# A two-layer diffusion step on TensorE: moving operands placed 16 bytes further on relative to the weights

## The chip, the cores and the metric

The kernel runs on one core of a Trainium2 chip, as one program in one launch. The metric is the device time of one execution in microseconds (us). A core has engines that run side by side: TensorE (PE in the profile; its weight loads are a row of their own, PEld), VectorE (DVE), ScalarE (ACT), GpSimd (POOL) and SyncE (SP), which issues the DMAs here.

## The reference

One inference step of a hybrid backbone of two layers, width 2048, for two groups of 128 tokens each: a context pass (`x_prompt`) and a denoising step (`x_sample`, which also attends to 128 cached keys). Both groups use the same weights, so the kernel carries them side by side as 256 columns.

```python
for l in range(DEPTH):                                   # DEPTH = 2
    mod = silu(cond) @ w_ada[l] + b_ada[l]               # 2048 x 12288
    sh1, sc1, gt1, sh2, sc2, gt2 = split(mod, 6)
    h = rmsnorm(x, g_norm_mix[l]) * (1 + sc1) + sh1
    x = x + gt1 * (mixer_ab(h) if l == 0 else mixer_c(h))
    h = rmsnorm(x, g_norm_ffn[l]) * (1 + sc2) + sh2
    x = x + gt2 * conv_ffn(h)
y = rmsnorm(x, g_final)
```

`mixer_ab` is multi-head latent attention beside grouped-query attention, with one input and one output projection. `mixer_c` is differential attention with eight heads. `conv_ffn` projects up to 2 x 5632 columns, convolves over three neighbouring tokens, multiplies the SiLU of one half with the other and projects down to 2048. All arrays are float32.

## The kernel before

Every weight matrix is cut into blocks of 128 x 128. A block arrives from memory as float32 in a tile `raw`, and `split` (lines 220 and 221) makes two tiles of it: ScalarE casts it to `wh` in the rounded format float32r, VectorE subtracts and writes the rest as `wl`. Activations are split in the same way into a high and a low half. A chunk product (`gemm`, lines 313, 314 and 317; `first_three`, lines 299 to 301, for the first three chunks after a norm) adds up three matmuls for each block: `wh` with the high half, `wh` with the low half, `wl` with the high half. The weights are the stationary operand, the activations the moving one, 256 columns of 4 bytes each time (384 in the products of latent keys and values). Each matmul has a weight load of its own, which runs beside the matmul before it.

The moving operands of all chunk products are five kinds of tiles:

- `hx`, 16 rows of 512 values (high half, low half) per partition: the normed and modulated input of each mixer and ConvFFN, and as `o` the heads' output of the first mixer (pool `keep`);
- `kv_in` and `ql`, latent keys and values and latent queries of the first mixer (pool `ab`);
- `oall`, the differential heads' output of the second mixer (pool `cc`);
- `g`, 22 tiles of 512 values, the gated product between the projections of the ConvFFN (pools `ffn0`, `ffn1`).

The weights `wh` and `wl` lie in four tiles each of 1024 values in the pool `wpool`, which follows `keep`. Tiles are allocated in the order in which their names first appear, at multiples of 32 bytes of each partition. Tiles named `pad` set where the next ones begin: 48 values ahead of the tiles of `wpool`, `SHIFT // 4` = 112 values ahead of `kv_in` and of the ConvFFN's tiles, `SHIFT // 4 - 24` ahead of `oall`. With them every moving tile starts 448 bytes (`SHIFT`) behind the weights, counted in a period of 512 bytes; rows, halves and blocks are multiples of 512 bytes apart.

The order of the work on each engine comes from a planner that simulates the program when it is built, apart from what is held in program order by hand. Between the chunk products a helper `pump` places the products for the modulation vectors (line 427 on TensorE, line 404 on VectorE) and steps of the attention heads. The chunk products of the two ConvFFN layers are the two long stretches (490 to 1215 us and 1650 to 2374 us); the first mixer lies before the one, the second mixer before the other.

```python
    T_(wpool, [P, 48], "pad", bufs=1)
    ...
                T_(ab, [P, SHIFT // 4], "pad")
                kv_in = T_(ab, [P, 4, 2, 3 * T], "kv_in", F32R)
    ...
        T_(cp, [P, SHIFT // 4 - 24], "pad")
        o_all = T_(cp, [P, KD, ROW], "oall", F32R)
```

Of the kernel before, what the change touches and what calls it, by code (L numbers as in the profile page):

```python
# [11 lines left out]
F32R = mybir.dt.float32r  # L12
# [6 lines left out]
P = 128  # L19
D = 2048  # L20
KD = D // P
T = 128
NT = 2 * T
ROW = 2 * NT
SHIFT = 448
NL = 2
GRID_W = 64
EPS = 1e-6
# [5 lines left out]
KQ = NFF // NQ  # L34
# [50 lines left out]
def step_kernel(ctx: ExitStack, tc: tile.TileContext, A: dict):  # L85
# [24 lines left out]
        return pl.tile(shape, dt, tag=tag, name=nm(tag), **kw)  # L110


    T_(wpool, [P, 48], "pad", bufs=1)


    cst = T_(keep, [P, NCONST], "cst")
# [410 lines left out]
    def modulated(st, l, which, W, fixed):  # L527


        ensure(l, 3 * which + 1)  # L530
        ensure(l, 3 * which)
        while later:
            later.pop(0)()
        u = ROWS[ada["i"]]
        tile_ = lambda t: T_(wpool, [P, 4, 512], "araw", bufs=2)

        def load_tile(t):
            raw = tile_(t)
            sp.dma_start(out=raw, in_=A["w_ada"][u[0], u[1], u[2], t])
            return raw  # L540

        raws = [load_tile(0), load_tile(1)]
        hx = T_(keep, [P, KD, ROW], "hx", F32R)
        r = stat_rstd(st, D, att_bank)
        sum_rows(0, raws[0], bank())
        rb = spread(diagonal(r, (0, 1)), bank=att_bank)
        sum_rows(1, raws[1])
        raws += [load_tile(2), load_tile(3)]
        modulate(hx, rb, l, which, range(KD), fixed)
        ada["i"] += 1  # L550
        rest = ada_finish(*u)

        def last_rows():
            sum_rows(3, raws[3])
            rest[0]()

        def turn():
            rest[1](tc.keep_in_program_order)

        ps = first_three(W, lambda k: hx[:, k, :NT], lambda k: hx[:, k, NT:2 * NT],  # L560
                         AS_MADE if fixed else IN_TURN, lambda: sum_rows(2, raws[2]), fixed)
        if fixed:
            W.ahead(lambda i: i)
        return hx, ps, [last_rows, turn]
# [72 lines left out]
    def mixer_ab(hx, rb0, st):  # L637
        l = 0
        with tc.tile_pool(name="ab", bufs=1) as ab:
            with tc.tile_pool(name="abp", bufs=1) as pj:  # L640
                T_(ab, [P, SHIFT // 4], "pad")
                kv_in = T_(ab, [P, 4, 2, 3 * T], "kv_in", F32R)
                ckc = T_(pj, [P, 4, T], "ckc")
                kr = T_(ab, [P, 3 * T], "kr")
                kg = T_(ab, [P, 2, 3 * T], "kg")
# [7 lines left out]
                    tc.keep_in_program_order(sp.dma_start(out=vg[:, 1], in_=A["cache_gqa_v"]))  # L653


                ql = T_(ab, [P, 6, 2 * NT], "ql", F32R)
                qb = T_(ab, [P, 8, NT], "qb")
                rsb = T_(ab, [P, 8, 2], "rsb")
                rsm = T_(ab, [P, 2], "rsmla")
# [131 lines left out]
            with tc.tile_pool(name="abh", bufs=1) as hp:  # L791
                ada["pew"] = PEW["heads"]

                o = T_(keep, [P, KD, ROW], "hx", F32R)
                load_cw(0)
                WQ = Weights(A["w_q_up"], 6, 2)
                WK = Weights(A["w_kv_up"], 4, 4)
                qh, qlo = (lambda k: ql[:, k, :NT]), (lambda k: ql[:, k, NT:])
                kh, klo = (lambda k: kv_in[:, k, 0]), (lambda k: kv_in[:, k, 1])
                qn, qr = {}, None  # L800

                def gqa_query(h):
                    s2 = T_(tmp, [P, NT], "sq", bufs=2)
                    act.activation(s2, qb[:, h], AF.Square)
                    act.activation(qb[:, h], qb[:, h], AF.Identity, scale=C("gqn"))
                    yield
                    pst = T_(pmisc, [P, 512], "misc")
                    for g in range(2):
                        pe.matmul(pst[:, g:g + 1], s2[:, g * T:(g + 1) * T], inv(128),
                                  start=True, stop=True)  # L810
                    rstd([pst[:, 0:2]], 2, HEAD_SCALE, rsb[:, h])
                    rope(qb[:, h:h + 1, T:], qb[:, h:h + 1, T:], 1, 64, "rch", "rsh")

                def gqa(h):
                    k = kg[:, h // 4]
                    return head_ab(hp, [(qb[:, h], k)], rsb[:, h], lambda b: vg[:, b, h // 4], o, 8 + h)

                def mla(h, qnh, qrh, knh, vh):
                    half = slice(64 * (h % 2), 64 * (h % 2) + 64)
                    return head_ab(hp, [(qnh, knh), (qrh[half], kr[half])], rsm,  # L820
                                   lambda b: vh[:, b], o, h)

                flush()
                start(gqa_query(0))
                for h in range(8):
                    if h % 2 == 0:
                        for i in range(2):
                            ps = gemm(WQ.chunk(), qh, qlo)
                            qn[h + i] = T_(hp, [P, NT], "qn", bufs=4)
                            act.copy(qn[h + i], ps)  # L830
                            pump(RATE["heads"])
                        ps = gemm(WQ.chunk(), qh, qlo)
                        ev = T_(tmp, [P, NT], "nt", bufs=4)
                        act.copy(ev, ps)
                        qr = T_(hp, [P, NT], "qr", bufs=2)
                        act.copy(qr[:, 0:T], ev[:, 0:T])
                        rope(qr[:, None, T:], ev[:, None, T:], 1, 32, "rcm", "rsm")
                        pump(RATE["heads"])
                    if h < 7:
                        start(gqa_query(h + 1))  # L840
                    start(gqa(h))
                    ps = gemm(WK.chunk(), kh, klo, 3 * T)
                    kn = T_(hp, [P, 3 * T], "kn", bufs=2)
                    act.copy(kn, ps)
                    pump(RATE["heads"])
                    ps = gemm(WK.chunk(), kh, klo, 3 * T)
                    vt = T_(hp, [P, 3 * T], "vt", bufs=2)
                    act.copy(vt, ps)
                    pump(RATE["heads"])

                    def values_and_head(h, vt, *a):
                        pt = T_(ppool["att"], [P, 512], "att", bufs=3)
                        for b in range(3):
                            pe.transpose(pt[:, b * T:(b + 1) * T], vt[:, b * T:(b + 1) * T], ident)
                        vm = T_(hp, [P, 3, P], "vm", bufs=2)
                        act.copy(vm.rearrange("p b d -> p (b d)"), pt[:, :3 * T])
                        yield
                        yield from mla(h, *a, vm)

                    start(values_and_head(h, vt, qn[h], qr, kn))  # L860
                flush()
# [11 lines left out]
    def mixer_c(cp, hx, W, ready, todo, st):  # L873
# [11 lines left out]

        xh, xl = (lambda k: hx[:, k, :NT]), (lambda k: hx[:, k, NT:2 * NT])
        product = lambda: ready.pop(0) if ready else gemm(W.chunk(), xh, xl, between=todo.pop(0) if todo else None)
        T_(cp, [P, SHIFT // 4 - 24], "pad")
        o_all = T_(cp, [P, KD, ROW], "oall", F32R)

        def project(h):
            q = T_(cp, [P, 2, NT], "dq", bufs=2)
# [103 lines left out]
    def ffn(hx, W, ready, todo, l, st):  # L996
# [4 lines left out]
        with tc.tile_pool(name=f"ffn{l}", bufs=1) as fp, banks(f"pffn{l}") as pf:  # L1001
# [22 lines left out]
            def up(q):  # L1024
                gs = []
                for i in range(q * KQ, (q + 1) * KQ):
                    rate = 0 if i < LATE else FRATE["up"]
                    fine[0] = False
                    gate = conv(i)
                    pump(0, rate)  # L1030
                    val = conv(NFF + i)
                    pump(0, rate)
                    act.activation(gate, gate, AF.Silu)
                    dve.tensor_tensor(out=val, in0=gate, in1=val, op=ALU.mult)
                    g = T_(fp, [P, ROW], "g", F32R, bufs=KQ)
                    split(g[:, :NT], g[:, NT:2 * NT], val)
                    gs.append(g)
                    if l == 0 and i == LATE - 1:
                        load_row()
                return gs  # L1040
# [18 lines left out]
    with banks("pab") as ppool["ada"]:  # L1059
        ppool["att"] = ppool["ada"]  # L1060
        for c in range(0, KD, 4):
            sp.dma_start(out=x[:, c:c + 4], in_=A["xT"][:, c:c + 4])
        first = {1: load_half(1, 0, "araw"), 0: load_half(0, 0, "raw")}
        ps = [bank(), att_bank()]
        for c in range(KD):
            sq = T_(tmp, [P, NT], "sq", bufs=2)
            act.activation(sq, x[:, c], AF.Square)
            for g in range(2):
                pe.matmul(ps[g][:, 0:1], sq[:, g * T:(g + 1) * T], inv(D), start=(c == 0), stop=(c == KD - 1))
        half_unit(1, 0, first[1], tc.keep_in_program_order)  # L1070
        rb0 = spread(diagonal(rstd([p[:, 0:1] for p in ps], 2), (0, 1)))
        half_unit(0, 0, first[0], tc.keep_in_program_order)
        hx = T_(keep, [P, KD, ROW], "hx", F32R)
        st = stat_init()
        mixer_ab(hx, rb0, st)
        W = Weights(A["w_up"][0], KD, 1)
        hx, ready, todo = modulated(st, 0, 1, W, False)
# [154 lines left out]
```

## Time and profile before

| | |
|---|---|
| median of 3 runs | 2377.19 us (2375.52 to 2379.86) |
| the profiled execution | 2375.77 us |
| its span, first to last instruction | 2374.0 us |
| TensorE busy | 2315.6 us (98%), 19626 instructions |
| weight loads | 2196.9 us (93%) |
| VectorE, ScalarE, GpSimd busy | 1799.1, 1172.7, 136.6 us |
| granted TensorE clock, mean | 0.989 of full |
| read from memory | 603.01 MB, 256 GB/s over the span |

The page of the profile lists the busy time of each engine, forty slices of the span, the chain of work that ended last, and groups of instructions: line, engine, operation, written tile, read tiles, shapes, count, then busy time, the mean duration of one in ns, and how long the engine was idle just before them. Matmuls overlap on TensorE: the duration of one is longer than the distance from its start to the next one's.

### The profile page before, as it was taken

The numbers are of one execution on the slowest core, as the hardware profiler recorded it, in microseconds if no ns is written. First come the engines' busy times: TensorE is split into PE (matmuls) and PEld (weight loads), VectorE is DVE, ScalarE is ACT, GpSimd is POOL, SyncE is SP. The second block draws the span as 40 slices with busy tenths as digits, with TensorE's granted clock in tenths as the row PEclk, the third lists the DMA queues.
The fourth block names the chain that finished last, engine by engine and source line by source line (L and its number), as shares of the span: only waits on it lengthen the run. The fifth ranks groups of instructions, "written<-read, shape, count | busy, mean of one in ns | idle before, by whom it ended". The sixth has DMA issues, their size and how long they took to land.

```text
span 2374.0 us, 47094 instructions
## 1 busy us (share of the span) xinstructions
PE 2315.6 (98%) x19626; PEld 2196.9 (93%) x19626; DVE 1799.1 (76%) x2677; ACT 1172.7 (49%) x1855; POOL 136.6 (6%) x132
## 2 busy tenths in 40 slices
PE   8899999999999999999999999998999999999997
PEld 6778868799999999999989999897999999999997
DVE  2667544479999999999968889799899755666654
ACT  4345544365554345554465555445555434555542
POOL 0001001110000000001220000022000000000011
PEclk9999999999999999999999999998999999999998
DMA  9886677877767876777767788776677555555553
GB/s 378 353 342 241 238 266 300 309 275 266 261 252 281 296 277 251 265 264 268 300 229 256 267 315 290 269 288 240 247 260 260 207 195 195 196 194 192 192 192 120
DMA packets 92405, 610.81 MB, mean 257 GB/s; under 512 B 9952, under 2 KB 17824, under 8 KB 20512
## 3 DMA queue, kind: packets, MB, share of 16 engines
q1 hardware_dynamic: 92192, 607.80, 69.6%
q8 instruction: 154, 2.52, 0.4%
q14 instruction: 59, 0.48, 0.1%
HBM read 603.01 MB, written 4.75 MB: 256 GB/s over the span
## 4 chain that ended last, share of the span: by engine, by line
PE 95%; DVE 2%; DMA 1%; issue 1%; ACT 1%; POOL 0%; POOLq 0%; DVEq 0%; ACTq 0%
PE acc L313 28%; PE acc L317 28%; PE acc L314 28%; PE ada L427 3%; DMA araw<-w_ada 1%; PE att L617 1%; PE acc L300 1%; PE acc L299 1%; PE acc L301 1%; PE misc L427 0%; PE att L934 0%; PE att L607 0%; DVE wl L221 0%; PE ada L340 0%; PE ada L376 0%
## 5 line engine op out<-in xcount | busy, mean ns | idle before, releaser
L220 ACT CAST wh<-raw 128x1024 fp32r<-128x1024 f32 (+1 forms) x788 | 794.0, 1013 | 943.1 <-PE acc L314 775.7
L221 DVE TENSOR_TENSOR wl<-raw,wh 128x1024 fp32r<-128x1024 f32 (+1 forms) x788 | 923.0, 1186 | 343.8 <-ACT wh L220 324.5
L313 PE MATMUL acc<-hx,wh 128*128 128x256 f32 x4064 | 1131.6, 279 | 9.7 <-ACT wh L220 4.2
L317 PE MATMUL acc<-hx,wl 128*128 128x256 f32 x4064 | 1127.8, 278 | 0.7 <-DVE wl L221 0.7
L314 PE MATMUL acc<-hx,wh 128*128 128x256 f32 x4064 | 1128.4, 278 | 0.0
L313 PEld LDWEIGHTS acc<-hx,wh 128*128 128x128 f32 x4064 | 764.7, 188 | 35.7 <-issue 13.3
L317 PEld LDWEIGHTS acc<-hx,wl 128*128 128x128 f32 x4064 | 765.0, 188 | 8.9 <-issue 6.7
L314 PEld LDWEIGHTS acc<-hx,wh 128*128 128x128 f32 x4064 | 765.3, 188 | 7.4 <-issue 6.9
L404 DVE CUSTOM_DVE_ANT_0 junk<-araw,condb 128x2048 f32<-128x2048 f32 (+1 forms) x184 | 424.8, 2309 | 1.1 <-DMA araw<-w_ada 1.1
L314 PE MATMUL acc<-g,wh 128*128 128x256 f32 x1408 | 388.3, 276 | 0.0
L317 PE MATMUL acc<-g,wl 128*128 128x256 f32 x1408 | 388.0, 276 | 0.0
L313 PE MATMUL acc<-g,wh 128*128 128x256 f32 x1408 | 387.8, 276 | 0.0
L314 PEld LDWEIGHTS acc<-g,wh 128*128 128x128 f32 x1408 | 264.3, 188 | 0.0
L317 PEld LDWEIGHTS acc<-g,wl 128*128 128x128 f32 x1408 | 264.2, 188 | 0.0
L313 PEld LDWEIGHTS acc<-g,wh 128*128 128x128 f32 x1408 | 264.1, 188 | 0.0
L175 POOL TENSOR_TENSOR sqacc<-sqacc,sq 128x256 f32<-128x256 f32 x62 | 80.7, 1302 | 1584.3 <-issue 1290.8
L1011 ACT ACTIVATE cv<-acc,convw 128x256 f32<-128x256 f32 x176 | 98.3, 559 | 2.8 <-PE acc L301 2.8
L569 DVE SCALAR_TENSOR_TENSOR x<-acc,mod,x 128x128 f32<-128x128 f32 x192 | 58.0, 343 | 49.2 <-PE acc L317 49.2
L427 PE MATMUL ada<-araw,condw 128*32 128x512 f32 x608 | 83.2, 624 | 6.0 <-DMA araw<-w_ada 5.0
L1017 DVE SCALAR_TENSOR_TENSOR cv<-acc,convw,cv 128x254 f32<-128x254 f32 x176 | 84.4, 480 | 3.7
L1014 DVE SCALAR_TENSOR_TENSOR cv<-acc,convw,cv 128x254 f32<-128x254 f32 x176 | 83.7, 476 | 2.2 <-ACT cv L1011 2.2
L313 PE MATMUL acc<-oall,wh 128*128 128x256 f32 x208 | 58.4, 281 | 2.3 <-DVE x L569 2.3
(229 smaller groups left out, 1789.8 us busy)
## 6 DMA issues: line engine op xcount, KB each, us to landing
araw<-w_ada SPq DMA_DIRECT2D x186, 1024.0 KB, 5.4
raw<-w_up SPq DMA_DIRECT2D x176, 1024.0 KB, 4.8
raw<-w_down SPq DMA_DIRECT2D x88, 1024.0 KB, 4.8
raw<-w_in_c SPq DMA_DIRECT2D x48, 1024.0 KB, 5.5
raw<-w_in_ab SPq DMA_DIRECT2D x19, 1024.0 KB, 7.1
raw<-w_out_ab SPq DMA_DIRECT2D x16, 1024.0 KB, 7.1
raw<-w_out_c SPq DMA_DIRECT2D x16, 1024.0 KB, 5.3
raw<-w_ada SPq DMA_DIRECT2D x6, 1024.0 KB, 10.8
```

Source lines behind the costliest of these rows:

```text
L175: pool.tensor_tensor(out=st["acc"], in0=st["acc"], in1=sq, op=ALU.add)
L220: pin(act.copy(out_hi, src))
L221: pin(dve.tensor_tensor(out=out_lo, in0=src, in1=out_hi.bitcast(F32), op=ALU.subtract))
L313: fixed(pe.matmul(ps[:, :n], wh, xh(k), start=(i == 0), stop=False))
L314: fixed(pe.matmul(ps[:, :n], wh, xl(k), start=False, stop=False))
L317: fixed(pe.matmul(ps[:, :n], wl, xh(k), start=False, stop=(i == last)))
L404: tc.keep_in_program_order(dve.tensor_tensor_reduce(out=junk, in0=raw, in1=condb[:, c].rearrange("p (g n) -> p g n", g=4), scale=1.0, scal ...
L427: i = pe.matmul(ada["ps"][32 * g:32 * g + 32, :], condw[:, 4 * t + g, :], raw[:, g], start=(t == 0), stop=(t == 3), skip_group_check=True)
L569: dve.scalar_tensor_tensor(out=x[:, c, s], in0=ps[:, s], scalar=mod[:, l, 3 * which + 2, c, g:g + 1], in1=x[:, c, s], op0=ALU.mult, op1=AL ...
L1011: pin(act.activation(y, ps, AF.Identity, scale=cw[:, 1, m:m + 1], bias=cw[:, 3, m:m + 1]))
L1014: pin(dve.scalar_tensor_tensor(out=y3[:, :, 1:], in0=p3[:, :, :T - 1], scalar=cw[:, 0, m:m + 1], in1=y3[:, :, 1:], op0=ALU.mult, op1=ALU.add))
L1017: pin(dve.scalar_tensor_tensor(out=y3[:, :, :T - 1], in0=p3[:, :, 1:], scalar=cw[:, 2, m:m + 1], in1=y3[:, :, :T - 1], op0=ALU.mult, op1=A ...
```

## The change

A constant `OFF = 4` (16 bytes) is added. A helper `placed` makes a tile that is 32 bytes longer than needed and returns the part that begins 16 bytes inside. The five kinds of moving tiles are made with it, or, for `g`, as a part of a tile that is 512 bytes longer than before. The pads shrink by 32 bytes where a tile that grew stands ahead, so that the weights stay where they were; a new tile `gap` ahead of `ql` makes its shift a multiple of 512 bytes plus 16. For `oall` the pad shrinks by 32 bytes and the part begins 16 bytes inside, so it starts 16 bytes earlier than before; the tiles behind it stay in place. Counted in 512 bytes, `hx`, `kv_in`, `ql` and `g` lie 464 bytes behind the weights, `oall` 432. Nothing is computed otherwise.

```diff
+OFF = 4
...
-    T_(wpool, [P, 48], "pad", bufs=1)
+    def placed(pl, n, tag, **kw):
+        return T_(pl, [P, n + 2 * OFF], tag, F32R, **kw)[:, OFF:OFF + n]
+
+    def rows(pl, tag):
+        return placed(pl, KD * ROW, tag).rearrange("p (k n) -> p k n", n=ROW)
+
+    T_(wpool, [P, 48 - 2 * OFF], "pad", bufs=1)
...
-        hx = T_(keep, [P, KD, ROW], "hx", F32R)
+        hx = rows(keep, "hx")
...
-                kv_in = T_(ab, [P, 4, 2, 3 * T], "kv_in", F32R)
+                kv_in = placed(ab, 4 * 2 * 3 * T, "kv_in").rearrange("p (k h n) -> p k h n", h=2, n=3 * T)
...
-                ql = T_(ab, [P, 6, 2 * NT], "ql", F32R)
+                T_(ab, [P, P - 2 * OFF], "gap")
+                ql = placed(ab, 6 * 2 * NT, "ql").rearrange("p (k n) -> p k n", n=2 * NT)
...
-                o = T_(keep, [P, KD, ROW], "hx", F32R)
+                o = rows(keep, "hx")
...
-        T_(cp, [P, SHIFT // 4 - 24], "pad")
-        o_all = T_(cp, [P, KD, ROW], "oall", F32R)
+        T_(cp, [P, SHIFT // 4 - 24 - 2 * OFF], "pad")
+        o_all = rows(cp, "oall")
...
-                    g = T_(fp, [P, ROW], "g", F32R, bufs=KQ)
+                    g = T_(fp, [P, ROW + P], "g", F32R, bufs=KQ)[:, OFF:OFF + ROW]
...
-        hx = T_(keep, [P, KD, ROW], "hx", F32R)
+        hx = rows(keep, "hx")
```

## The prediction

> **What bounds the kernel now.** I read the page first: span, shares, chain, groups.
>
> ```profile
> span 2374.0 us, 47094 instructions
> PE 2315.6 (98%) x19626; PEld 2196.9 (93%) x19626; DVE 1799.1 (76%) x2677; ACT 1172.7 (49%) x1855; POOL 136.6 (6%) x132
> PEclk9999999999999999999999999998999999999998
> PE 95%; DVE 2%; DMA 1%; issue 1%; ACT 1%; POOL 0%; POOLq 0%; DVEq 0%; ACTq 0%
> PE acc L313 28%; PE acc L317 28%; PE acc L314 28%; PE ada L427 3%; DMA araw<-w_ada 1%; PE att L617 1%; PE acc L300 1%; PE acc L299 1%; PE acc L301 1%; PE misc L427 0%; PE att L934 0%; PE att L607 0%; DVE wl L221 0%; PE ada L340 0%; PE ada L376 0%
> L313 PE MATMUL acc<-hx,wh 128*128 128x256 f32 x4064 | 1131.6, 279 | 9.7 <-ACT wh L220 4.2
> L317 PE MATMUL acc<-hx,wl 128*128 128x256 f32 x4064 | 1127.8, 278 | 0.7 <-DVE wl L221 0.7
> L314 PE MATMUL acc<-hx,wh 128*128 128x256 f32 x4064 | 1128.4, 278 | 0.0
> ```
>
> TensorE is the chain: 95% of it is PE, 84% the three matmuls of the chunk products (L313, L314, L317), at a granted clock that is full nearly throughout, and the last column says that PE sits idle before them for about 10 us in all. So the time is the number of these matmuls times the distance from one start to the next. The mean of 279 ns is not that distance, because matmuls overlap; it has to be read from starts. The timeline gives them, in two places:
>
> ```profile
> 560.05 0.28 PE L313 MATMUL acc<-hx,wh 128*128 128x256 f32 x1
> ...
> 599.83 0.28 PE L313 MATMUL acc<-hx,wh 128*128 128x256 f32 x1
> 1559.76 0.28 PE L313 MATMUL acc<-oall,wh 128*128 128x256 f32 x1
> ...
> 1599.69 0.28 PE L313 MATMUL acc<-oall,wh 128*128 128x256 f32 x1
> 560.00:600.00 40.00, 32.46 (x118) 22.09 (x118) 1.00 0.68 244
> 1560.00:1600.00 40.00, 31.75 (x114) 21.29 (x114) 1.00 0.78 284
> ```
>
> The last two lines are the windows view for line L313 alone (length, PE busy and count, weight loads, clock, DMA). The quoted pair at 560 us is the first and the last of 118 L313, so 117 steps of three matmuls: 39.78 us / 117 = 0.340 us, 113.3 ns a matmul. At 1560 us the first and the last of 114 are 113 steps apart: 39.93 us / 113 = 0.353 us, 117.8 ns. Same instruction, same shape, clock 1.00 in both: **two rhythms, 4.5 ns apart**, and the slow one lasts. The mean durations show which rhythm a stretch is in (groups kept by shape, for four windows, in the order 490 to 1215, 1527 to 1650, 336 to 490 and 1215 to 1527 us):
>
> ```profile
> L317 PE MATMUL acc<-hx,wl 128*128 128x256 f32 x1360 | 375.6, 276 | 0.0
> L317 PE MATMUL acc<-g,wl 128*128 128x256 f32 x704 | 193.8, 276 | 0.0
> L317 PE MATMUL acc<-oall,wl 128*128 128x256 f32 x208 | 58.2, 281 | 0.0
> L317 PE MATMUL acc<-hx,wl 128*128 128x256 f32 x251 | 69.8, 279 | 0.0
> L317 PE MATMUL acc<-hx,wl 128*128 128x256 f32 x720 | 201.5, 280 | 0.0
> 0.00:490.00 490.00, 220.86 (x760) 144.07 (x760) 0.98 0.79 302
> 490.00:1215.00 725.00, 569.21 (x2064) 387.38 (x2064) 1.00 0.73 270
> 1215.00:1650.00 435.00, 261.72 (x928) 174.70 (x928) 0.98 0.75 271
> 1650.00:2374.00 724.00, 569.35 (x2064) 387.31 (x2064) 0.99 0.58 206
> ```
>
> 276 ns is the fast rhythm, 281 the slow one, 279 and 280 are mixtures (a few long ones after an interruption lie in them). Both ConvFFN layers, 490 to 1215 and 1650 to 2374 us, are in the fast rhythm throughout. The last four rows count L313 by stage: 760 + 2064 + 928 + 2064 = 5816; three matmuls each, 17,448, of which 192 are the 384-column ones of the latent keys and values. A change of 1 ns in the distance is worth 17 us.
>
> **The change part by part.** In the allocation of the kernel before, the weights (wh, wl) start at byte 32 of a 512-byte period and all five moving tiles at byte 480: the moving operand lies 448 bytes on, SHIFT's value. Rows of hx are 2048 bytes apart, its low half 1024 behind the high one, weight blocks 512 apart, so the pairs that meet on PE differ by all multiples of 512, and the three lines show the same 276 ns: a multiple of 512 makes no difference. The change makes the distance 464 for hx, g, kv_in and ql, and 432 for oall, whose pad shrinks by 32 bytes before its 16 are added. The pitch of g grows by 512 bytes and ql moves by 528; by the same argument that counts as 16.
>
> No instruction, wait or DMA is added, removed or put past another on any queue; SBUF has the room (the pool cc ends where it did). What can change is (a) the distance between matmuls, (b) the writes that make these tiles. For (b) these rows, all of the first ConvFFN layer:
>
> ```profile
> L221 DVE TENSOR_TENSOR g<-cv,g 128x256 fp32r<-128x256 f32 x44 | 18.3, 416 | 0.0
> L220 ACT CAST g<-cv 128x256 fp32r<-128x256 f32 x44 | 17.4, 396 | 0.6 <-DVE cv L1034 0.4
> 490.00:1215.00 725.00, 722.40 (x6343) 716.67 (x6342) 654.94 (x837) 363.94 (x486) 30.88 (x22) 1.00 0.73 270
> ```
>
> The writes of g take 18 us of VectorE and 17 us of ScalarE there. VectorE is busy 655 of 725 us (third pair of the last row), so 70 us are free; even if these writes took twice as long, 18 us would fit, and PE waits for VectorE's weight halves 0.7 us in the whole kernel (L317 above). If that cover were gone, the price would be those 18 us a layer. Taken: 0.
>
> For (a) no row has another distance than 448, so the cost is bounded by the rows of matmuls that meet their weight loads differently. Upwards: the sustained slow rhythm, +4.5 ns. The FFN layers have 2 x 2064 x 3 = 12,384 matmuls in the fast one; all of them slow is +56 us, and the stages that are now mixed would add up to 15 us when wholly slow (5064 matmuls, 3 ns at most). Downwards, this row of the attention's value product, whose weight loads are of the same 188 to 192 ns:
>
> ```profile
> L632 PEld LDWEIGHTS att<-pT,vg x16: 190/192/192, 241.4 to 356.0; 128*128 128x128 f32 x16
> L632 PE MATMUL att<-pT,vg x16: 275/275/275, 241.5 to 356.1; 128*128 128x128 f32 x16
> L376 PEld LDWEIGHTS ada<-cst,am x80: 137/141/143, 60.1 to 1542.5; 128*128 128x128 f32 x80
> L376 PE MATMUL ada<-cst,am x80: 270/272/332, 60.1 to 1542.6; 128*128 128x128 f32 x80
> ```
>
> 275 ns against 276: 1 ns, 17,448 x 1 = 17 us, and with the slow stretches gone some 10 us more (oall's 624 matmuls at 5 ns, 3 us; about half of the mixed 2160 + 753 at 5 ns, 7 us): -27 us. The transposes' 272 ns would be -4 ns, -70 us, but their weight loads take 141 ns and ours 188, so I take L632. [...]
>
> The ends are -27 and +71 us. Which way 16 bytes go cannot be read from a row. Two things weigh: the downside of the two rhythms is three times the upside, since the FFN layers stand in the better one already; and where hx meets its weights between many interruptions (336 to 490 and 1215 to 1527 us), the stream falls into either rhythm, which says that 448 lies near an edge between them. I take the row nearest to that, the mixture: half of the FFN matmuls in the slow rhythm, 12,384 x 0.5 x 4.5 ns = **+28 us**, the other stages as now. The profiled execution took 2375.77 us (span 2374.0), 1.4 below the median of 2377.19; on the median the forecast is 2377 + 28 = **2405 us**.
>
> **The rivals.**
>
> *Faster: the matmuls get out of the weight loads' way.* The distance falls from 113.3 ns by the 1 ns that L632 has, and the slow rhythm vanishes: 2377 - 27 = 2350 us. For it: tiles are allocated in multiples of 32 bytes, so 448 is one point of a coarse row and a better place may lie between two of them; and L632 shows such loads beside shorter matmuls. Against: at most 1 ns is shown for loads of this length. It decides for the whole kernel from the first FFN product at 490 us on, since nothing interrupts the stream there.
>
> *Neutral: 16 bytes do not matter.* Both rhythms stay where they are, only the mixed stages lock otherwise: a few us either way, 2372 to 2382, middle 2377. For it: the moving rows start at a multiple of 16 bytes before and after, and multiples of 512 do nothing. Against: two rhythms of one instruction at one clock show that something besides the columns sets the distance, and it is not waiting for another engine (idle 0.0). [...]
>
> *Slower by all of it.* Every chunk product goes to 117.8 ns: +71, 2448 us; the far end of the forecast's own case.
>
> That the change doesn't do what it says needs a period other than 512, under which g and ql would move by more; the equal 276 ns of L313, L314 and L317 speak against it, and I give it no chance of its own.
>
> **How the numbers follow.** Forecast's case (more matmuls in a slow rhythm) 0.46, own range 2383 to 2440; faster 0.37; neutral 0.17. A measurement of this kernel can tell about 0.2% (4.8 us) from no change; of the neutral case 0.13 lie within, 0.02 on each side. So faster 0.37 + 0.02 = 0.39, same 0.13, slower 0.46 + 0.02 = 0.48. The range runs from the faster case's 2350, less 3 for the uncertain share of slow stretches, 2347, to 2440; that leaves out the last of the slow end (all FFN matmuls and the mixed stages slow, about 0.12) and a gain beyond L632's 1 ns (about 0.06).
>
> **What would show it.** In the profile after, the groups kept by shape for 490 to 1215 us: forecast, the mean of L313, L314, L317 on hx or g goes from 276 to 278 or 279 (a mixture, or one of the layers at 281), with idle before them still near 0, and VectorE's busy time unchanged; faster, 275 and counts above 118 in 40 us; neutral, 276 and 118. The writes of g should stay at 416 and 396 ns. oall, which moves the other way, tells whether the sign of the step matters: above 281, worse; at 276, better. The prediction is wrong if both FFN layers keep 276 ns or less; also if the distance stays and PE's idle time before L313 grows, which would make it VectorE's or ScalarE's doing.

## The result: 2465 us, 3.65% slower

The changed kernel takes 2465.24 us (median of 4 runs, 2462.08 to 2466.31) against 2378.2 us of the kernel before (4 runs): ratio 1.0365, 95% interval 1.0347 to 1.0383. That is 87 us more, outside the range that was forecast, on the side that was forecast.

The page of the profile after, the lines that answer to those shown of before (the change moved the numbers of the lines by 7: L313, L314, L317 are now L320, L321, L324):

```profile
span 2464.5 us, 47094 instructions
PE 2404.2 (98%) x19626; PEld 2288.9 (93%) x19626; DVE 1804.6 (73%) x2677; ACT 1167.0 (47%) x1855; POOL 141.2 (6%) x132
PEclk9999999999999999999999999998999999999998
L320 PE MATMUL acc<-hx,wh 128*128 128x256 f32 x4064 | 1154.2, 285 | 9.7 <-ACT wh L227 4.2
L324 PE MATMUL acc<-hx,wl 128*128 128x256 f32 x4064 | 1150.9, 284 | 0.7 <-DVE wl L228 0.7
L321 PE MATMUL acc<-hx,wh 128*128 128x256 f32 x4064 | 1151.5, 284 | 0.0
```

The instructions are the same in number, the clock is the same, VectorE and ScalarE have the same work, and TensorE is idle before the chunk products as little as before (9.7 and 0.7 us). What changed is the distance from one matmul to the next. The timeline of the first ConvFFN layer gives the distance (first and last L320 of the window from 560 to 600 us), the windows view the count, and the groups kept by shape (490 to 1260 us) the durations; the last line, from the page, is the product of the tile that moved the other way:

```profile
559.93 0.28 PE L320 MATMUL acc<-hx,wh 128*128 128x256 f32 x1
...
599.97 0.28 PE L320 MATMUL acc<-hx,wh 128*128 128x256 f32 x1
560.00:600.00 40.00, 31.61 (x113) 21.14 (x113) 1.00 0.68 240
L324 PE MATMUL acc<-hx,wl 128*128 128x256 f32 x1360 | 384.4, 283 | 0.0
L320 PE MATMUL acc<-g,wh 128*128 128x256 f32 x704 | 198.5, 283 | 0.0
L228 DVE TENSOR_TENSOR g<-cv,g 128x256 fp32r<-128x256 f32 x44 | 18.3, 417 | 0.0
L227 ACT CAST g<-cv 128x256 fp32r<-128x256 f32 x44 | 17.4, 395 | 0.0
L320 PE MATMUL acc<-oall,wh 128*128 128x256 f32 x208 | 59.3, 286 | 2.2 <-DVE x L576 2.2
```

113 starts are 112 steps of three matmuls: 40.04 us / 112 = 0.3575 us, **119.2 ns a matmul**, where it was 113.3. This is neither of the two rhythms of the profile before, but a third one, slower than both, and both ConvFFN layers run in it from end to end. Between the two profiled executions (2466.31 and 2375.77) lie 90.5 us. Both kernels run the 19626 matmuls in the same order, so the times to the next start can be compared one by one: the 12,384 products of the FFN layers took 72 us more (5.8 ns each), the 5064 of the mixers 16 us (3.2 ns each), the 576 products of `first_three` 4.5 us, and everything else 2.4 us less. The writes of g (the DVE and ACT rows) take what they took.

### The profile page after: what moved, and what is told of

It is laid out like the page before. It is cut to its first block, busy times and chain, and to the rows that moved or that the text cites. A ratio compares the mean times of both kernels' runs of the same rounds, so it can differ in the third digit from the quotient of the medians.

```text
span 2464.5 us, 47094 instructions
## 1 busy us (share of the span) xinstructions
PE 2404.2 (98%) x19626; PEld 2288.9 (93%) x19626; DVE 1804.6 (73%) x2677; ACT 1167.0 (47%) x1855; POOL 141.2 (6%) x132
## 4 chain that ended last, share of the span: by engine, by line
PE 95%; DVE 2%; DMA 2%; issue 1%; ACT 1%; POOL 0%; POOLq 0%; DVEq 0%; ACTq 0%
PE acc L320 28%; PE acc L324 28%; PE acc L321 28%; PE ada L434 3%; DMA araw<-w_ada 1%; PE acc L307 1%; PE att L624 1%; PE acc L306 1%; PE acc L308 1%; DVE wl L228 0%; PE att L942 0%; PE misc L434 0%; PE att L614 0%; PE ada L347 0%; PE ada L383 0%
## 5 line engine op out<-in xcount | busy, mean ns | idle before, releaser
L320 PE MATMUL acc<-hx,wh 128*128 128x256 f32 x4064 | 1154.2, 285 | 9.7 <-ACT wh L227 4.2
L324 PE MATMUL acc<-hx,wl 128*128 128x256 f32 x4064 | 1150.9, 284 | 0.7 <-DVE wl L228 0.7
L321 PE MATMUL acc<-hx,wh 128*128 128x256 f32 x4064 | 1151.5, 284 | 0.0
L320 PEld LDWEIGHTS acc<-hx,wh 128*128 128x128 f32 x4064 | 769.2, 189 | 35.6 <-issue 13.7
L324 PEld LDWEIGHTS acc<-hx,wl 128*128 128x128 f32 x4064 | 770.0, 190 | 8.9 <-issue 6.7
L321 PEld LDWEIGHTS acc<-hx,wh 128*128 128x128 f32 x4064 | 770.4, 190 | 7.4 <-issue 6.9
L321 PE MATMUL acc<-g,wh 128*128 128x256 f32 x1408 | 397.5, 283 | 0.0
L324 PE MATMUL acc<-g,wl 128*128 128x256 f32 x1408 | 397.3, 283 | 0.0
L320 PE MATMUL acc<-g,wh 128*128 128x256 f32 x1408 | 397.1, 283 | 0.0
L321 PEld LDWEIGHTS acc<-g,wh 128*128 128x128 f32 x1408 | 266.3, 189 | 0.0
L324 PEld LDWEIGHTS acc<-g,wl 128*128 128x128 f32 x1408 | 266.2, 189 | 0.0
L320 PEld LDWEIGHTS acc<-g,wh 128*128 128x128 f32 x1408 | 266.1, 189 | 0.0
L182 POOL TENSOR_TENSOR sqacc<-sqacc,sq 128x256 f32<-128x256 f32 x62 | 86.2, 1391 | 1654.5 <-issue 1353.4
L320 PE MATMUL acc<-oall,wh 128*128 128x256 f32 x208 | 59.3, 286 | 2.2 <-DVE x L576 2.2
```

The costliest lines, as they stand in the source:

```text
L182: pool.tensor_tensor(out=st["acc"], in0=st["acc"], in1=sq, op=ALU.add)
L320: fixed(pe.matmul(ps[:, :n], wh, xh(k), start=(i == 0), stop=False))
L321: fixed(pe.matmul(ps[:, :n], wh, xl(k), start=False, stop=False))
L324: fixed(pe.matmul(ps[:, :n], wl, xh(k), start=False, stop=(i == last)))
```

## The experiments

There are three theories. **Theory 1**: the distance between moving operand and weights alone sets the rhythm, inside TensorE. **Theory 2**: a moving operand that starts off a boundary of 32 bytes costs more, wherever the weights lie. **Theory 3**: something else that came with the change costs (larger tiles, the pitch of g, the writes).

### One part alone: g

```diff
-                    g = T_(fp, [P, ROW], "g", F32R, bufs=KQ)
+                    g = T_(fp, [P, ROW + P], "g", F32R, bufs=KQ)[:, OFF:OFF + ROW]
```

> The kernel before, with only g moved 16 bytes on (pitch 2560). Theory 1: only the 4224 products that read g go from 113.3 to 119.2 ns, +25 us, ratio 1.0105; hx stays at 276 ns. Theory 3: any other split.

2401.38 against 2375.83 us: ratio 1.0108, interval 1.0093 to 1.0123. The page of this run (its L314 is L313 of the kernel before):

```profile
L314 PE MATMUL acc<-hx,wh 128*128 128x256 f32 x4064 | 1132.3, 279 | 10.2 <-ACT wh L221 4.8
L314 PE MATMUL acc<-g,wh 128*128 128x256 f32 x1408 | 397.1, 283 | 0.0
```

The products of hx stay at 279 ns, those of g go from 276 to 283. The loss is 25.5 us, against 25 worked out from 4224 matmuls: the cost follows the moved tile.

### All of the change but the 16 bytes

```diff
-    def placed(pl, n, tag, **kw):
-        return T_(pl, [P, n + 2 * OFF], tag, F32R, **kw)[:, OFF:OFF + n]
+    def placed(pl, n, tag, at=0, **kw):
+        return T_(pl, [P, n + 2 * OFF], tag, F32R, **kw)[:, at:at + n]
...
-        o_all = rows(cp, "oall")
+        o_all = rows(cp, "oall", 2 * OFF)
...
-                    g = T_(fp, [P, ROW + P], "g", F32R, bufs=KQ)[:, OFF:OFF + ROW]
+                    g = T_(fp, [P, ROW + P], "g", F32R, bufs=KQ)[:, :ROW]
```

> The changed kernel with its larger tiles, smaller pads, gap and pitch, but the moving operands at the start of their places, distance 448 again for all five kinds. Theory 1 (distance alone): ratio 1.000, 113.3 ns and 276 ns in the long stretches. Theory 3 (the layout or the writes cost): some of the 87 us stays, ratio up to 1.037.

2375.96 against 2376.75 us: ratio 0.999, interval 0.9966 to 1.0015; its page has g back at 276 ns:

```profile
L320 PE MATMUL acc<-g,wh 128*128 128x256 f32 x1408 | 387.8, 276 | 0.0
```

Tile sizes, pads, gap and pitch cost nothing that can be measured; theory 3 falls.

### 32 bytes instead of 16

```diff
-OFF = 4
+OFF = 8
```

> The changed kernel with OFF = 8: moving operands 32 bytes on, distance 480 (oall 416). Theory 2 (start off a 32-byte boundary): as fast as before, ratio 1.00, 276 ns in the long stretches. Theory 1 (distance): as slow as at 464 or slower, ratio 1.03 to 1.08, unless the curve turns within 32 bytes. Theory 3 (larger tiles and pitch, other writes): ratio 1.037 as with 16 bytes.

2453.69 against 2375.83 us: ratio 1.0331, interval 1.0314 to 1.0349. From its page:

```profile
L320 PE MATMUL acc<-hx,wh 128*128 128x256 f32 x4064 | 1148.8, 283 | 9.6 <-ACT wh L227 4.2
L320 PE MATMUL acc<-g,wh 128*128 128x256 f32 x1408 | 394.8, 281 | 0.0
```

Both g and hx start at multiples of 32 bytes again and are slow all the same, so theory 2 falls as it was put. The distance of 480 bytes is nearly as bad as 464: the products of g stand 118.3 ns apart in this trace.

### The matmuls alone, over all distances

Bursts replace the step: the same three matmuls over eight blocks, five times, with the other engines idle from 11 us on and the start of the moving operand as the only thing that differs. Each burst writes a tile with a name of its own.

```diff
+    def burst(name, off, woff=0, times=5):
...
+            h = wh[:, woff + k * P:woff + (k + 1) * P]
+            l = wl[:, woff + k * P:woff + (k + 1) * P]
+            xh = m[:, off + k * ROW:off + k * ROW + NT]
+            xl = m[:, off + k * ROW + NT:off + k * ROW + 2 * NT]
+            pin(pe.matmul(ps[:, :NT], h, xh, start=(i == 0), stop=False))
+            pin(pe.matmul(ps[:, :NT], h, xl, start=False, stop=False))
+            pin(pe.matmul(ps[:, :NT], l, xh, start=False, stop=(i == n - 1)))
...
+    for i in range(32):
+        burst(label("up", i), 4 * i)
```

The offsets count values of 4 bytes, so a step is 16 bytes. Bursts `up` go upwards, `dn` downwards, `br` upwards once more with four wide matmuls ahead of each.

> Not the step but bursts of its matmuls alone: 120 matmuls (wh with the high half, wh with the low half, wl with the high half, eight blocks five times) for each of 32 distances of the moving operand behind the weights, 0 to 496 bytes in steps of 16, with no other engine at work; upwards, downwards, and upwards once more with four wide matmuls ahead of each burst. Theory 1, the distance alone sets the rhythm inside TensorE: about 113.3 ns from start to start (mean duration 276 ns) at 448, about 119.2 ns at 464, and a curve over the distance. Theory 2, a moving operand that starts off a 32-byte boundary costs more wherever the weights lie: 113.3 at every even step, 119 at every odd one. Theory 3, the loss comes from the rest of the kernel (the writes of VectorE and ScalarE, the larger pitch of g): one value at all distances.

The answers for the tiles of four bursts, upwards at 448, 464 and 480 bytes and at 448 behind the wide matmuls (line, form, count: shortest, median and longest duration in ns, first and last start in us):

```profile
L132 PE MATMUL upbc<-m,wh x40: 276/276/282, 406.7 to 420.0; 128*128 128x256 f32 x40
L132 PE MATMUL upbd<-m,wh x40: 278/282/288, 420.3 to 434.2; 128*128 128x256 f32 x40
L132 PE MATMUL upbe<-m,wh x40: 277/280/285, 434.6 to 448.4; 128*128 128x256 f32 x40
L132 PE MATMUL brbc<-m,wh x40: 281/281/384, 1347.2 to 1361.1; 128*128 128x256 f32 x40
```

40 starts are 39 steps of three matmuls: 13.3 us / 117 is 114 ns, 13.9 us / 117 is 119, 13.8 us / 117 is 118. The starts in full resolution give, for the later half of each burst upwards, the time from start to start in ns:

| distance, bytes | 0 | 16 | 32 | 48 | 64 | 80 | 96 | 112 | 128 | 144 | 160 | 176 | 192 | 208 | 224 | 240 |
|---|---|---|---|---|---|---|---|---|---|---|---|---|---|---|---|---|
| ns | 120.0 | 118.7 | 116.7 | 118.3 | 117.8 | 120.0 | 120.0 | **113.3** | 118.7 | 118.7 | 117.3 | 119.2 | **113.3** | 119.2 | 118.3 | 117.2 |

From 256 to 496 bytes the row repeats to 0.1 ns: the period is 256 bytes, 448 is the place 192, 464 the place 208. Bare matmuls at these two have the kernel's 113.3 and 119.2 ns, and at 480 the 118.3 of the run with 32 bytes, so the loss needs no other engine. 448 stands alone: its neighbours on both sides, 16 bytes away, cost 119.2. The last fence line shows the two rhythms of the profile before: behind the wide matmuls the burst at 448 settles at 281 ns (117.8 from start to start) and stays there. The burst at 192 does the same; at 112 and 368 all three passes end at 113.3.

> The same bursts with the weights moved too: first weights 16 bytes on and the moving operand 0 to 496 bytes behind them, then weights 32 bytes on in the same way, then weights in place and the distance from 384 to 512 in steps of 4 bytes. Theory 1 (distance alone): the same curve as with the weights in place, so 113.3 ns at a distance of 448 although the moving operand then starts at an odd multiple of 16. Theory 2 (the moving operand's own boundary of 32 bytes): with weights 16 bytes on, the slow and the fast steps change places, 119 ns at 448 and 113.3 at 464. In steps of 4 bytes theory 1 expects either a smooth passage from 113.3 to 119.2 between 448 and 464 or a step at one of them.

With the weights 16 bytes on and the moving operand at an odd multiple of 16, the distance 448 has 113.3 ns and 464 has 123.3 (`sabc`, `sabd`); with the weights 32 bytes on, 113.3 and 119.2 again:

```profile
L132 PE MATMUL sabc<-m,wh x40: 275/275/281, 410.2 to 423.5; 128*128 128x256 f32 x40
L132 PE MATMUL sabd<-m,wh x40: 281/286/292, 423.8 to 438.3; 128*128 128x256 f32 x40
L132 PE MATMUL sbbd<-m,wh x40: 278/282/288, 877.5 to 891.4; 128*128 128x256 f32 x40
```

Theory 2 had the fast and the slow step change places; they do not. But the distance is not all: 112 bytes, fast with weights at a multiple of 32, has 120.0 ns with the weights 16 further. The place of the pair within 32 bytes counts as well, so what stays of theory 1 is that the places of the two operands set the rhythm, and not their distance alone.

> Bursts alone again: the distance from 0 to 252 bytes in steps of 4, first with the weights at a multiple of 32 bytes, then 16 bytes further on. Theory 1 (distance sets the rhythm, with a period of 256 bytes as the sweep by 16 showed): 113.3 ns at 112 and 192 bytes in the first row and at 192 in the second, and at the few other steps that the coarse sweep stepped over, 144 among them (400 less 256); between 116 and 124 ns elsewhere. Open: whether any step falls below 113.3 ns. If the reads of weights and moving operand only collide at some steps, a step without collisions should show it, at 109 to 112 ns; if 113.3 is the floor of the weight load, none does.

In steps of 4 bytes, with the weights at a multiple of 32, 113.3 ns stands at 64, 112, 144 and 192 bytes alone; the 60 other places have 116.7 to 124.4. The passage beside 192 is a step: 118.5 ns at 188, 121.7 at 196. With the weights 16 bytes on only 64 and 192 are fast. In the sweep by 16, places 64 and 144 had 117.8 and 118.7: like 192 they have more than one rhythm. **No place measured is below 113.3.** The two ends of the expectation's 109 to 112 ns stand in the profile before, at matmuls of 128 columns: the transposes (L376) start 109 ns apart, those of L632 112 (medians).

### What the distance acts on

These are bursts again, now with other widths of the moving operand (`n_`), or with 256 columns that repeat the same few (`same`).

```diff
-            xh = m[:, off + k * ROW:off + k * ROW + NT]
+            xh = m[:, off + k * ROW:off + k * ROW + n_]
...
+            xh, xl = (v if same is None else m[:, off:off + same][:, None, :].to_broadcast([P, n_ // same, same]) for v in (xh, xl))
```

> Bursts with other widths of the moving operand at 448 and 464 bytes (2, 64, 128, 192, 224, 256, 320, 384, 448, 512 columns), then 256 columns that repeat 4, 64 or 128 of them, and 256 columns with one and the same weight block. If the weight load is what ends last at 448, narrow moving operands stay at one distance (111 to 113 ns) and the start-to-start time grows only above 256 columns. If reads of the two operands collide, the repeated 4 columns (one 16-byte place of memory) take another time than 256 different ones, and do not depend on where they start by more than one step; at 464 the loss against 448 grows with the width up to 256 columns and stays above it, since the weight load reads only so long. If neither: the same values at all forms.

First 224 columns at 448 and 464, then 256, then 256 that repeat 4 columns at 448 and 464, then 256 that repeat 64:

```profile
L135 PE MATMUL waae<-m,wh x40: 270/274/288, 190.7 to 203.8; 128*128 128x224 f32 x40
L135 PE MATMUL wbae<-m,wh x40: 273/273/276, 204.1 to 217.2; 128*128 128x224 f32 x40
L135 PE MATMUL waaf<-m,wh x40: 276/276/293, 217.5 to 230.8; 128*128 128x256 f32 x40
L135 PE MATMUL wbaf<-m,wh x40: 278/282/288, 231.2 to 245.1; 128*128 128x256 f32 x40
L135 PE MATMUL sxaa<-m,wh x40: 273/274/275, 428.5 to 441.6; 128*128 128x256 f32 x40
L135 PE MATMUL sxab<-m,wh x40: 272/274/275, 482.8 to 495.9; 128*128 128x256 f32 x40
L135 PE MATMUL syaa<-m,wh x40: 276/276/282, 442.0 to 455.2; 128*128 128x256 f32 x40
L135 PE MATMUL syab<-m,wh x40: 278/281/288, 496.2 to 510.2; 128*128 128x256 f32 x40
```

From the starts: 192 and 224 columns take 111.7 ns at either distance, so there the time depends neither on the width nor on the distance. The weight load of 128 columns is what all have in common; that it sets the 111.7 ns is not shown. 256 columns take 113.3 and 119.2, 320 columns 146.7 and 153.3, 384 columns 174.7 and 176.7, 448 columns 202.2 and 204.0, 512 columns 233.3 and 234.7. So the loss is 5.9 ns at 256 columns, 6.6 at 320, and only 1.4 to 2.0 from 384 on. The expectation from colliding reads was that it stays above 256 columns; it did not, and why is open. 256 columns that repeat the same 16 bytes take 112.0 at 448, 464 and 0, 112.4 at 480: hardly any dependence is left. 256 columns that repeat 64 of them, 256 bytes, take the same as 256 different ones, 113.3 and 119.2, which agrees with the period of 256 bytes in the sweep. One and the same weight block instead of eight changes nothing: 276 ns at 448 and 282 at 464 (median durations of `swaa` and `swab`), as with eight. So the loss at 464 stood at 256 columns and more, not at 192 and 224, and was gone where 256 columns repeat 16 bytes. Why is not shown; that the reads of the two operands collide was the author's guess in the expectation, and no record shows a collision.

### A further place, and another order of columns

In the kernel before, the weights are put 256 bytes on, so that the distance is 192:

```diff
-SHIFT = 448
+SHIFT = 192
...
-    T_(wpool, [P, 48], "pad", bufs=1)
+    T_(wpool, [P, 112], "pad", bufs=1)
```

> The kernel before with the weights moved 256 bytes on (pad of 112 values, SHIFT = 192): distance 192 for all five kinds. Theory 1 with the period of 256 bytes from the sweep: 113.3 ns, 276 ns mean duration in the long stretches, ratio 1.000. With a period of 512 bytes: another rhythm, ratio 1.02 to 1.05. If the place in SBUF and not the distance counted, any ratio but 1.000.

2375.5 against 2375.69 us, ratio 1.000, interval 0.999 to 1.0009. The period of 256 bytes holds for the kernel.

The changed kernel with the weights 96 bytes on (`SHIFT = 352`, a pad of 64 values, none ahead of oall):

> All moving operands 368 bytes behind the weights (oall 112), the place of the sweep that had 113.3 ns in all its passes, also right behind an interruption, where 448 and 192 fell into 117.8. If this carries over to the kernel, the slow rhythm goes from the mixers: long stretches as before at 276 ns, the stages from 200 to 490 us and from 1215 to 1650 us shorter by some 9 us together (2.0 thousand starts at 117.9 instead of 113.3), ratio 0.996. If the two rhythms come from the interruptions and not from the place: ratio 1.000.

2376.6 against 2376.75 us: ratio 0.9992, interval 0.9971 to 1.0012. The gain that was forecast, 9 us, did not come. It had all 2006 starts of the profile before that lie between 116 and 125 ns become fast; in this run's trace 1115 are left, 654 of them at 119 to 121 ns, a rhythm that the bursts at this place did not end in. 900 starts by 4.5 ns would be 4 us, under what these runs can tell. And the 2006 are themselves no fixed number: the kernels at the place 192 of the runs above, with distances of 448 (larger tiles, no 16 bytes) and 192, have 1530 and 1444 in their traces. In the stretch of oall's product alone (1527 to 1650 us) there are 651 in the profile before, 218 and 62 in those two, and 41 here. The product of oall, at 281 ns in the profile before, stands in the pages of the three runs so (448 with larger tiles, 192, 368):

```profile
L320 PE MATMUL acc<-oall,wh 128*128 128x256 f32 x208 | 57.7, 278 | 2.3 <-DVE x L576 2.3
L313 PE MATMUL acc<-oall,wh 128*128 128x256 f32 x208 | 57.5, 277 | 1.2 <-DVE x L569 1.2
L320 PE MATMUL acc<-oall,wh 128*128 128x256 f32 x208 | 58.1, 280 | 2.2 <-DVE x L576 2.2
```

So the slow rhythm of oall in the profile before is not fixed by the place: other executions with the same place do without most of it. What 368 changed beyond that is mixed: from 1215 to 1527 us 386 slow starts against 824 to 895 in the three traces at the place 192, up to 490 us 624 against 402 to 510.

The last run goes back to bursts and changes the order in which the columns are read: four columns (16 bytes) from each of four stretches in turn, or pieces of other sizes (`line` values of 4 bytes):

```diff
+            turn = lambda v: v.rearrange("p (s j e) -> p j s e", e=line, s=NT // per)
+            xh, xl = turn(xh), turn(xl)
```

> Bursts at distances 0 to 240 in steps of 16 bytes, with the 256 columns read in another order: four columns (16 bytes) from each of four stretches that lie 256 bytes apart before the next four; with the results put back in place in PSUM (first row) or left in the new order (second row); then in pieces of 8 and of 32 bytes, and from two stretches 512 bytes apart. If the collisions come from where in a period of 256 bytes the two reads stand, the order changes the rhythm at each distance and the best place moves; a row with a step at 111.7 ns, the bound of the weight load, would point to a faster kernel (17.4 thousand products by 1.6 ns, 28 us). If the first row is slower than the second, scattered writes to PSUM cost.

No order reaches 113.3 ns. The 111.7 ns that the expectation calls the bound of the weight load are the time of 192 and 224 columns; that the load sets it is the author's reading. Pieces of 16 bytes from four stretches take 133.3 to 138.9 ns, the same with the results scattered in PSUM (where TensorE writes its sums) or not; pieces of 8 bytes 223.3 to 226.7; pieces of 32 bytes 117.2 to 128.9; pieces of 16 bytes from two stretches 123.3 to 129.6. Only pieces of 32 bytes are anywhere clearly faster than columns in a row at the same distance, at 96 bytes (117.8 against 120.0). No order tried and no place measured points to a kernel faster than the one before.

## Why the prediction was wrong

**What held.** The bound held (TensorE's start-to-start distance, in it everything but some us), and so did the reading of the rhythm from the mean duration and the free parts: VectorE's and ScalarE's writes of g stayed at 417 and 395 ns, layout and pitch cost nothing (ratio 0.999), multiples of 512 bytes count for nothing (276 ns at L313, L314 and L317 alike). The direction came true too, but no row had shown it: of the two things that were weighed for it one did not hold (below), so it was in part luck.

**The step that failed** is the bound upwards in part (a), and with it the value taken. The prediction priced the loss by the only slower rhythm that the trace showed, +4.5 ns, and called all matmuls in it the far end; it then took half of the FFN's matmuls, +28 us. Measured: a third rhythm, +5.9 ns from start to start, in all of them, +72 us there; the mixers, put at no change, took 16 us more, and the 576 products of `first_three`, which the count of 17,448 leaves out, 4.5 us more. At +4.5 ns the far end was 71 us, so even that end was too low. The two rhythms of one distance are no sample of the rhythms of other distances: the sweeps have values from 113.3 to 124.4 ns, most of them between 117 and 121. The mixture was the wrong row too: the FFN layers went as a whole from one rhythm, 113.3 ns, to one other, 119.2. The mixture stands in stages with many interruptions, at a place for which the bursts show two rhythms, 113.3 ns and, behind wide matmuls, 117.8. Nor do interruptions alone make a mixture: the FFN layers are interrupted as well (L427, 32 matmuls between 490 and 1215 us), other than the prediction says, and came back to 113.3 ns.

**The weighing.** "448 lies near an edge between the two rhythms" was right in the sense that both exist at 448, but the edge does not lie in the distance: the neighbours at 444 and 452 bytes have neither. None of the 128 places measured is below the 113.3 ns of 448, so the faster rival had no room: L632's 275 ns (its starts are 112 ns apart) belong to loads beside 128 columns.

**The rivals.** *Neutral* falls: the same bare matmuls go from 113.3 to 119.2 ns when the moving operand moves by 16 bytes, with the other engines idle. For 256 columns of 4 bytes the measurement decides against a time that does not depend on where the two operands lie; what in TensorE or its memory makes it depend on that is not shown. *Slower by all of it* came nearest: every kind of chunk product did get slower, but its term was too small, 4.5 for 5.9 ns. *Faster* has nothing: 113.3 is the lowest value in every sweep, 1.6 ns above the 111.7 that narrower matmuls reach. For oall, 432 bytes (place 176, 119.2 ns in the sweep) is as bad as 464: its mean went to 286 ns, 119.3 from start to start, so the sign of the step did not matter.

## What to carry to other kernels

Where a stream of matmuls is the whole time and each has its own weight load, read the distance from start to start and compare it with what the same load reaches beside a narrower matmul (here 113.3 and 119.2 ns at 256 columns, 111.7 at 192 and 224); a difference of a few ns with no idle time may come from where the two operands lie to each other, as the 5.9 ns did here. Such places are worth a sweep with bare matmuls before anything is moved: here they showed the neighbours of 448 (119.2 ns on both sides), the period of 256 bytes and the lowest value, 113.3. A place that was found good is an optimum until shown otherwise, and the trace of that place alone does not bound what the next one costs.

## What the runs showed of the hardware

- The start-to-start time of the bursts' matmuls of 256 float32r columns, each with its weight load, depended on the distance of the two operands in SBUF (the memory on the core that holds the tiles): from 0 to 240 bytes it went from 113.3 to 120.0 ns, and from 256 to 496 bytes the values came again to 0.1 ns. With the weights at a multiple of 32 bytes it was 113.3 ns at 4 of 64 places and 116.7 to 124.4 at the others, with another value 4 bytes further on (118.5 at 188, 113.3 at 192, 121.7 at 196); with the weights 16 bytes further, 113.3 at 2 of 64.
- The place 192 had two stable rhythms, 113.3 and 117.8 ns. In the bursts the one behind wide matmuls took the slow one and kept it to its end; in the kernel the same product, oall's, ran at 281 ns in one execution and at 277 or 278 in others with the same place.
- In the bursts of 128, 64 and 2 columns, float32r matmuls took 213.3 ns from start to start, longer than at 192 or 224 (111.7); their weight loads lasted 333 ns beside 128 columns and 192 ns beside 192. The kernel's float32 matmuls of 128 columns (L632) show no such step: their starts are 112 ns apart (median).
- A moving operand of 256 columns read in pieces of 16 bytes from four stretches in turn took 133 to 139 ns, from two stretches 123 to 130, and in pieces of 8 bytes from four stretches 223 to 227; columns in a row at these distances took 113.3 to 120.0. Why the time grows so much from pieces of 16 bytes to pieces of 8 no run shows.
